# Attention scores with keys on partitions, and two heads side by side on 64 rows of TensorE

## The chip, the cores and the metric

The kernel runs on one core of one Trainium2 chip. The metric is the device time of one execution in microseconds (us), and a lower number is better. One profiled execution, taken by the hardware profiler, gives the trace from which all rows below come.

## The reference

One layer of a hybrid encoder is computed for one sequence of 1024 tokens with 1024 features, in float32. A gated linear recurrence (branch A) and an attention (branch B) are projected from the same normed input, each is gated and projected, their sum goes through an output projection, and a convolutional feed-forward block follows. The change touches the attention alone, which has 8 query heads of 64 features, 2 key/value heads, and no mask:

```python
def gqa_bidirectional(aq, ak, av, q_norm_g, k_norm_g):
    ...
    q = apply_axial_rope(q, tabs) * (AT_HD ** -0.5)
    k = apply_axial_rope(k, tabs)
    ...
    def block(qblk):
        s = jnp.einsum('bqkgd,bskd->bkgqs', qblk, k)
        p = jax.nn.softmax(s, axis=-1)
        return jnp.einsum('bkgqs,bskd->bqkgd', p, v)
```

So every query's scores against all 1024 keys are computed, their maximum is taken off, the exponential is taken, divided by its sum, and multiplied with the values.

## The kernel before

Precision: the TensorE products run on the type `float32r`, which drops low bits of a float32. So each float32 operand is kept as two such halves, a high one (h) and a low one (l), and a product is summed from several partial products. `split` (L76) makes the halves: ScalarE copies the source to h (L77), VectorE subtracts h from the source to get l (L78). `mm3` (L91) issues the products hh, hl and lh.

Order of the stages: projections and the recurrence; the query, key and value projections with their normalisation and rotation (`rope_unit`, L455), from which `finish_q` (L505) and `finish_k` (L496) make transposed halves; the attention; the gated projections of the two branches (L639 on); the output projection; the feed-forward block.

Before the change, `qT[h]` (L427) holds one head: 64 rows of high halves above 64 rows of low halves. `kT[g][0]` holds a key head's high halves twice, one copy below the other, `kT[g][1]` the low halves twice. So one matmul over 128 rows sums two partial products at once.

The attention goes over 32 units (L589 to L603). A unit is a pair of heads (four pairs) and a block of 128 queries (eight blocks). `scores(u, j)` (L540) computes, for one head j of the pair, the scores of 128 queries (on the partitions) against 1024 keys (along a row): four matmuls of 512 columns (L547, L548). VectorE takes each row's maximum (L550), ScalarE the exponential with the maximum as bias and the row sum as a by-product (L553), VectorE the reciprocal (L554), and VectorE scales the row (L555). `turn(u, j)` (L558) then transposes the probabilities on TensorE, eight blocks of 128x128 (L567), because the product with the values needs the keys on partitions, and splits the transposed blocks into halves. `values(u)` (L570) multiplies them with `vv`, which holds for each key block the high and the low half of the values side by side: 16 matmuls of 256 columns (L578). The two halves' results are added (L582 to L586).

TensorE's order is pinned by hand (`pin`, L532). Between these steps `fill(n)` (L535) issues the next n matmuls of ten branch-gate projections (`gate_steps`, L249; 48 matmuls of 512 columns each), which depend on nothing in the attention. The other engines' order is set by the scheduler of the framework, and the DMAs are issued from one queue (SP). PSUM has 8 banks; pool `gps` holds three of them for projections.

## Time and profile before

| what | us |
|---|---|
| median of 3 runs (1615.79 to 1616.55) | 1616.35 |
| the profiled execution | 1616.18 |
| its span, first to last instruction | 1614.3 |
| attention, from the first score matmul (469.5) to the first gated projection (764.5) | 295.0 |

A row of the timeline or of a group names the engine (PE is TensorE's matmuls, PEld its weight loads, DVE is VectorE, ACT is ScalarE, SP issues DMAs), the line of the kernel, the operation, the tiles as out<-in, and the shapes. A matmul's "128\*128 128x512" is the weights' rows and columns and then the output's partitions and columns; the time given for a matmul is a modelled latency, and since matmuls are pipelined, what one costs in a stream is the distance from its start to the next one's.

### The profile page before, as it was taken

How to read it: one execution, taken by the hardware profiler on the slowest of the kernel's cores; microseconds unless marked ns; L12 is line 12 of the kernel's file. 1: busy time of each engine (PE TensorE's matmuls, PEld its weight loads, DVE VectorE, ACT ScalarE, POOL GpSimd, SP SyncE). 2: the span in 40 equal slices, each digit the busy share in tenths (PEclk: the TensorE clock that was granted, in tenths of full speed). 3: DMA queues.
4: the chain of work that ended last, by engine and by line, in shares of the span. 5: the costliest groups of instructions: out<-in, count | busy, mean ns of one | idle time of the engine just before them, and what ended most of it. 6: DMA issues, size and time to landing. Idle time of an engine off the chain costs nothing.

```text
span 1614.3 us, 21171 instructions
## 1 busy us (share of the span) xinstructions
PE 1579.3 (98%) x8376; PEld 1334.1 (83%) x8376; DVE 1112.5 (69%) x1632; ACT 768.0 (48%) x1204; POOL 35.3 (2%) x33
## 2 busy tenths in 40 slices
PE   8999999999999999999999989999999999999998
PEld 7988998888988888888788877788788888787887
DVE  5366465534758888888654288887888777967576
ACT  5375454513555666656432344544544444444432
POOL 0000000000000000000000052000000000000000
PEclk9999999999999999999999999999999999999999
DMA  5011111121110101102445111322222224685343
GB/s 204 27 41 38 53 40 49 64 78 54 46 60 27 46 33 40 47 26 99 167 140 195 53 59 66 104 98 98 98 98 98 103 106 147 212 296 186 100 122 104
DMA packets 59764, 150.34 MB, mean 93 GB/s; under 512 B 6161, under 2 KB 6417, under 8 KB 59666
## 3 DMA queue, kind: packets, MB, share of 16 engines
q1 hardware_dynamic: 59666, 148.99, 26.9%
q8 instruction: 66, 1.08, 0.3%
q14 instruction: 32, 0.26, 0.1%
HBM read 109.91 MB, written 39.06 MB: 92 GB/s over the span
## 4 chain that ended last, share of the span: by engine, by line
PE 85%; DVE 6%; DMA 5%; ACT 3%; issue 1%; SPq 0%; DVEq 0%; ACTq 0%
PE pa L741 13%; PE gp L257 10%; PE pc L741 6%; PE pv L578 4%; PE pb L741 3%; PE pt L567 3%; PE s L547 2%; PE hp L93 2%; PE s L548 2%; PE hp L94 2%; PE hp L92 2%; PE y L93 2%; PE y L94 2%; PE y L92 2%; PE wo L94 2%; PE wo L93 2%
## 5 line engine op out<-in xcount | busy, mean ns | idle before, releaser
L77 ACT CAST pth<-pt 128x512 fp32r<-128x512 f32 x128 | 71.1, 589 | 77.8 <-PE pt L567 77.5
L77 ACT CAST dz<-dr 128x512 fp32r<-128x512 f32 (+1 forms) x66 | 50.6, 767 | 102.1 <-PE da L94 35.8
L78 DVE TENSOR_TENSOR dz<-dr,dz 128x512 fp32r<-128x512 f32 (+1 forms) x66 | 56.9, 867 | 50.8 <-ACT dz L77 50.6
L78 DVE TENSOR_TENSOR ptl<-pt,pth 128x512 fp32r<-128x512 f32 x128 | 84.0, 683 | 10.3 <-ACT pth L77 9.9
L257 PE MATMUL gp<-uT1h,w_g 128*128 128x512 f32 x256 | 86.9, 398 | 0.0
L257 PE MATMUL gp<-uT0h,w_g 128*128 128x512 f32 x256 | 86.4, 400 | 0.0
L550 DVE TENSOR_REDUCE m<-s 128x1 f32<-128x1024 f32 x64 | 78.3, 1224 | 7.3 <-PE s L548 6.3
L553 ACT ACTIVATE p<-s,m 128x1024 f32<-128x1024 f32 x64 | 72.1, 1127 | 19.7 <-DVE m L550 19.7
L741 PE MATMUL pc<-c1t,wb 128*128 128x512 f32 x264 | 69.5, 398 | 5.5 <-ACT c1t L77 5.0
L741 PE MATMUL pa<-c0b,wa 128*128 128x512 f32 x264 | 68.9, 394 | 2.8 <-ACT wa L77 1.7
L741 PE MATMUL pb<-c0b,wa 128*128 128x512 f32 x264 | 68.7, 390 | 0.5 <-DVE ta L714 0.5
L567 PEld LDWEIGHTS pt<-cs,p 128*128 128x128 f32 x512 | 58.7, 140 | 12.0 <-issue 4.8
L741 PE MATMUL pa<-c1t,wb 128*128 128x512 f32 x264 | 67.9, 395 | 0.0
L567 PE MATMUL pt<-cs,p 128*128 128x128 f32 x512 | 66.9, 273 | 0.5 <-DVE p L555 0.5
L578 PE MATMUL pv<-pth,vv 128*128 128x256 f32 x256 | 65.1, 292 | 0.0
L741 PEld LDWEIGHTS pc<-c1t,wb 128*128 128x128 f32 x264 | 50.5, 192 | 17.0 <-ACT c1t L77 5.2
L77 ACT CAST wc<-r 128x1024 fp32r<-128x1024 f32 x22 | 23.1, 1052 | 86.1 <-PE pc L741 76.4
L578 PE MATMUL pv<-ptl,vv 128*128 128x256 f32 x256 | 62.5, 282 | 0.0
L741 PEld LDWEIGHTS pa<-c0b,wa 128*128 128x128 f32 x264 | 49.0, 188 | 15.4 <-ACT wa L77 3.2
L741 PEld LDWEIGHTS pa<-c1t,wb 128*128 128x128 f32 x264 | 50.1, 190 | 12.0 <-DVE c1t L78 0.4
L741 PEld LDWEIGHTS pb<-c0b,wa 128*128 128x128 f32 x264 | 49.5, 188 | 11.4 <-DVE ta L714 0.9
L868 DVE SCALAR_TENSOR_TENSOR cv<-c,vc,cv 128x1023 f32<-128x1023 f32 x44 | 56.3, 1279 | 2.6 <-ACT cv L867 2.6
(461 smaller groups left out, 4578.1 us busy)
## 6 DMA issues: line engine op xcount, KB each, us to landing
r<-in_wup_dram SPq DMA_DIRECT2D x44, 512.0 KB, 3.3
left_d<-cv SPq DMA_DIRECT2D x33, 512.0 KB, 3.2
dr<-left_d SPq DMA_DIRECT2D x66, 256.0 KB, 2.7
raw_g<-in_win_f_dram SPq DMA_DIRECT2D x16, 512.0 KB, 3.2
gate_d<-gt SPq DMA_DIRECT2D x32, 256.0 KB, 2.0
gl<-gate_d SPq DMA_DIRECT2D x16, 512.0 KB, 4.0
raw_h<-in_win_f_dram SPq DMA_DIRECT2D x12, 512.0 KB, 3.3
w<-in_wdown_dram SPq DMA_DIRECT2D x20, 256.0 KB, 5.4
```

The costliest lines, as they stand in the source:

```text
L77: S.copy(h, src)
L78: V.tensor_tensor(out=l, in0=src, in1=h.bitcast(F32), op=ALU.subtract)
L92: T.matmul(ps, ah, bh, start=first, stop=False, skip_group_check=more)
L93: T.matmul(ps, ah, bl, start=False, stop=False, skip_group_check=more)
L94: return T.matmul(ps, al, bh, start=False, stop=last, skip_group_check=more)
L257: yield T.matmul(ps, a[:, w], b[:, k, :], start=k == 0 and n == 0, stop=k == KT - 1 and n == 2)
L550: V.tensor_reduce(out=m, in_=s, axis=AX.X, op=ALU.max, negate=True)
L553: S.activation(pb, s, AF.Exp, bias=m, accum_out=z)
L567: pin(T.transpose(pt[:, i, :], pb[:, k * P:(k + 1) * P], ident))
L578: pin(T.matmul(pv, vv[pair // 2][:, k, :], pts[u][k // 4][n][:, k % 4, :, :], start=k == 0 and n == 0, stop=k == KT - 1 and n == 1))
L741: T.matmul(ps, a[:, k * P:(k + 1) * P], x[:, k, :], start=first and n == 0, stop=n == len(seq) - 1, skip_group_check=not first)
L868: V.scalar_tensor_tensor(out=cv[:, 1:], in0=src[:, :-1], scalar=w0, in1=cv[:, 1:], op0=ALU.mult, op1=ALU.add)
```

## The change

The scores are computed the other way round, with 128 keys on the partitions and 512 queries along a row, so that no probabilities need transposing. `qT[pair]` now is a high tile and a low tile, each with the pair's first head on rows 0 to 63 and its second head on rows 64 to 127; `finish_q` splits per pair. The attention is 8 units u (a pair and a half of the queries) of 8 steps n (a block of 128 keys):

- `maxima(n)` is a first pass with queries on partitions, on the high halves alone: two matmuls of 64 rows, one per head, and a VectorE maximum over 2x512. After eight of these, `max_row(u)` transposes the maxima into one row per head (partitions 0 and 64). The first pass runs 12 steps ahead (`LEAD`).
- `scores(n)` issues three partial products (hh, lh, hl) for each of the two heads, on 64 rows each, and then for each head a matmul of one row of ones with the row of negated maxima, which subtracts the maximum. ScalarE takes the exponential of both heads, and `split` makes the halves.
- `values(n)` multiplies with the values, four matmuls of 512 columns over all 128 rows, and VectorE adds the step's probabilities to a running sum.
- `norm(u)`, ten steps later, sums that over the partitions with four matmuls against ones; the sums go through DRAM (`z_d`), are inverted, come back spread over partitions, and scale the output of a pair. It is run for every unit; the trip to DRAM and back is made once per pair.
- `fill` is called with 6 after each of the first 12 maxima, 10 before the loop, 3 and 2 in each step, 24 after it, and the rest behind the last `norm`.
- The PSUM pool `gps` is closed ahead of the attention and its work there goes through two banks of `mps`; the pool `mp` of the stage behind is opened only when the attention's own pool is closed.

The functions `scores`, `turn` and `values` of before and their loop are removed; three places where a `gps.tile` call is written as `psg` are left out below.

```diff
@@ -57,9 +57,11 @@
     dram = ctx.enter_context(tc.tile_pool(name="dram", bufs=1, space=bass.MemoryType.DRAM))
     gstack = ExitStack()
     gps = pool("gps", 3, gstack, space=PSUM)
+    psg = lambda name: gps.tile([P, 512], F32, tag="g", name=name)
     oa_d = dram.tile([HG_HEADS, P, L], F32, name="oa_d")
     gate_d = dram.tile([2 * KT, P, L], F32, name="gate_d")
+    z_d = dram.tile([4, 2, 2, L], F32, name="z_d")
     h_d = dram.tile([8, P, D], F32, name="h_d")
     left_d = [dram.tile([7, P, NH], F32, name=f"left_d{k}") for k in range(NFF // 2)]
@@ -424,7 +426,7 @@
     slot_q = lambda name, dt=F32R: slot(apq, "q", 8, name, dt)
     slot_k = lambda name, dt=F32R: halves(apk.tile([P, 2, L], dt, tag="k", name=name, bufs=2))
     slot_v = lambda name, dt=F32R: halves(apk.tile([P, 2, L], dt, tag="v", name=name))
-    qT = [slot_q(f"qT{h}") for h in range(AT_HEADS)]
+    qT = [[slot_q(f"q{n}{r}") for n in "hl"] for r in range(AT_HEADS // 2)]
     kT = [slot_k(f"kT{g}") for g in range(2)]
     vv = [v.rearrange("p (a b) -> p a b", b=P) for v in slot_v("vv")]
@@ -504,30 +506,39 @@
     def finish_q(base):
         def f(a, t0, n, name):
-            st = rp.tile([P, 4, n, 2, HD], F32R, tag="st", name=f"st{name}{t0}", bufs=2)
-            split(st[:, :, :, 0, :], st[:, :, :, 1, :], a)
-            for h in range(4):
-                transposed(st[:, h].rearrange("p n a e -> p n (a e)"), qT[base + h], t0, n, f"{name}{h}{t0}")
+            st = rp.tile([P, 2, 2, n, 2, HD], F32R, tag="st", name=f"st{name}{t0}", bufs=2)
+            for r in range(2):
+                both = lambda z: z.rearrange("p n a e -> p a n e")
+                split(both(st[:, 0, r]), both(st[:, 1, r]), a[:, 2 * r:2 * r + 2])
+                for z in range(2):
+                    transposed(st[:, z, r].rearrange("p n a e -> p n (a e)"), qT[base + r][z], t0, n, f"{name}{z}{r}{t0}")
         return f
     rope_unit(unit_t(4, "kv"), 2, tabs[1], finish_k, "k", vsplit=True)
     rope_unit(unit_t(5, "q0"), 4, tabs[0], finish_q(0), "q0")
-    end = rope_unit(unit_t(6, "q1"), 4, tabs[0], finish_q(4), "q1")
+    end = rope_unit(unit_t(6, "q1"), 4, tabs[0], finish_q(2), "q1")
     with tc.issue_after(end.ins):
         for c in range(NG0, NG0 + NG1):
             gate_proj(c)
     pr.close()
-    mn = ExitStack()
-    mp = pool("mp", 1, mn, side="right")
+    gstack.close()
+    mn, ob0 = ExitStack(), ExitStack()
+    mo = pool("mo", 1, ob0, side="right")
+    slot_o = lambda name, dt=F32R: slot(mo, "ob", 1, name, dt)
+    ast = ExitStack()
+    mp = pool("mpa", 1, ast, side="right")
     mps = pool("mps", 1, at, space=PSUM)
-    slot_t = lambda name, dt=F32R: slot(mp, "pt", 8, name, dt)
-    slot_p = lambda name, dt=F32R: slot(mp, "p", 2, name, dt)
-    slot_o = lambda name, dt=F32R: slot(mp, "ob", 1, name, dt)
+    psg = lambda name: mps.tile([P, 512], F32, tag="g", name=name, bufs=2)
+    ps2 = lambda name: mps.tile([P, 2, 512], F32, tag="s", name=name, bufs=2)
     obT = []
-    probs, pts = {}, {}
     fills = (m for c in range(NG0 + NG1, 2 * KT) for m in gate_steps(c))
+    NU = 8
+    heads = (slice(0, HD), slice(HD, P))
     def pin(ins):
         tc.keep_in_program_order(ins)
@@ -536,75 +547,139 @@
         for m in itertools.islice(fills, n):
             pin(m)
...
+    mneg, mrow = {}, {}
+    def maxima(n):
+        u, qt, hf = n // 8, n % 8 // 2, n % 2
+        pair, c = u // 2, u % 2
+        if n % 8 == 0:
+            mneg[u] = mp.tile([P, 4, 2, 2], F32, tag="mneg", name=f"mneg{u}", bufs=2)
+        o = c * 512 + qt * P
+        ps = ps2(f"x{n}")
+        for i, r in enumerate(heads):
+            pin(T.matmul(ps[:, i, :], qT[pair][0][r, o:o + P], kT[pair // 2][0][r, hf * 512:(hf + 1) * 512],
+                         start=True, stop=True))
+        V.tensor_reduce(out=mneg[u][:, qt, hf, :], in_=ps, axis=AX.X, op=ALU.max, negate=True)
+        if n % 8 == 7:
+            V.tensor_tensor(out=mcol[:, :, 0:HD + 1:HD], in0=mneg[u][:, :, 0, :], in1=mneg[u][:, :, 1, :], op=ALU.min)
+    def max_row(u):
+        pt = psg(f"mt{u}")
+        for t in range(4):
+            pin(T.transpose(pt[0:HD + 1, t * P:(t + 1) * P], mcol[:, t, :], ident))
+        mrow[u] = mp.tile([P, 512], F32R, tag="mrow", name=f"mrow{u}", bufs=2)
+        S.copy(mrow[u][0:HD + 1, :], pt[0:HD + 1, :])
+    probs, accs = {}, {}
+    def scores(n):
+        u, kt = n // 8, n % 8
+        pair, c = u // 2, slice(u % 2 * 512, u % 2 * 512 + 512)
+        kh, kl = (z[:, kt * P:(kt + 1) * P] for z in kT[pair // 2])
+        qh, ql = qT[pair]
+        ps = ps2(f"s{n}")
+        for j, (a, b) in enumerate(((kh, qh[:, c]), (kh, ql[:, c]), (kl, qh[:, c]), (ones, mrow[u]))):
+            for i, r in enumerate(heads):
+                w = slice(r.start, r.start + 1) if j == 3 else r
+                pin(T.matmul(ps[:, i, :], a[w, :], b[w, :], start=j == 0, stop=j == 3))
+        p = mp.tile([P, 2, 512], F32, tag="p", name=f"p{n}", bufs=5)
+        S.activation(p, ps, AF.Exp)
+        ph, pl = (mp.tile([P, 2, 512], F32R, tag=f"p{z}", name=f"p{z}{n}", bufs=2) for z in "hl")
+        split(ph, pl, p)
+        probs[n] = ph, pl, p
+    def add_to(acc, p):
+        V.tensor_tensor(out=acc, in0=acc, in1=p, op=ALU.add)
+    pvs = {}
+    def values(n):
+        u, kt = n // 8, n % 8
+        pair = u // 2
+        if kt == 0:
+            pvs[u] = [mps.tile([P, 512], F32, tag="v", name=f"pv{u}{i}", bufs=2) for i in range(2)]
+            if u % 2 == 0:
+                obT.append((slot_o if pair == 0 else slot_q)(f"obT{pair}", F32))
+        for i in range(2):
+            for z, p in enumerate(probs[n][:2]):
+                pin(T.matmul(pvs[u][i], vv[pair // 2][:, kt, :], p[:, i, :], start=kt == 0 and z == 0, stop=kt == 7 and z == 1))
+        p = probs.pop(n)[2]
+        if kt == 0:
+            accs[u] = p
         else:
-            fill(8)
+            add_to(accs[u], p)
+        if kt < 7:
+            return
+        c = slice(u % 2 * 512, u % 2 * 512 + 512)
+        f = mp.tile([P, 512], F32, tag="f", name=f"f{u}")
+        for i, r in enumerate(heads):
+            S.copy(f[r, :], pvs[u][i][heads[1 - i], :])
+        for i, r in enumerate(heads):
+            V.tensor_tensor(out=obT[pair][r, c], in0=pvs[u][i][r, :], in1=f[r, :], op=ALU.add)
+    def norm(u):
+        pair, c = u // 2, slice(u % 2 * 512, u % 2 * 512 + 512)
+        ah, al = (mp.tile([P, 2, 512], F32R, tag=f"p{z}", name=f"a{z}{u}", bufs=2) for z in "hl")
+        split(ah, al, accs.pop(u))
+        z = psg(f"z{u}")
+        for i in range(2):
+            for j, a in enumerate((ah, al)):
+                pin(T.matmul(z, side[:, (1 - i) * P:(2 - i) * P], a[:, i, :], start=i + j == 0, stop=i + j == 2))
+        zs = mp.tile([P, 512], F32, tag="f", name=f"zs{u}")
+        S.copy(zs, z)
+        for i in range(2):
+            nc.sync.dma_start(z_d[pair, 0, i:i + 1, c], zs[i * HD:i * HD + 1, :])
+        if u % 2 == 0:
+            return
+        rz = mp.tile([P, 16], F32, tag="rz", name=f"rz{u}")
+        flat = lambda a: a.rearrange("i (p w) -> (i p) w", w=16)
+        nc.sync.dma_start(rz, flat(z_d[pair, 0]))
+        V.reciprocal(rz, rz)
+        nc.sync.dma_start(flat(z_d[pair, 1]), rz)
+        rb = mp.tile([P, L], F32, tag="p", name=f"rb{u}", bufs=5)
+        for i, r in enumerate(heads):
+            nc.sync.dma_start(rb[r, :], z_d[pair, 1, i:i + 1, :].to_broadcast([HD, L]))
+        V.tensor_tensor(out=obT[pair], in0=obT[pair], in1=rb, op=ALU.mult)
+    one_f = mp.tile([P, 512], F32, tag="f", name="one_f")
+    nc.gpsimd.memset(one_f[:, 0:4 * HD], 0.0)
+    nc.gpsimd.memset(one_f[:, HD:3 * HD], 1.0)
+    side = mp.tile([P, 4 * HD], F32R, name="side")
+    S.copy(side, one_f[:, 0:4 * HD])
+    ones = side[:, HD:3 * HD]
+    mcol = mp.tile([P, 4, HD + 1], F32, name="mcol")
+    nc.gpsimd.memset(mcol, 0.0)
+    LEAD = 12
+    for n in range(LEAD):
+        maxima(n)
+        fill(6)
+        if n == 8:
+            max_row(0)
+    scores(0)
+    fill(10)
+    for n in range(8 * NU):
+        if n + 1 < 8 * NU:
+            scores(n + 1)
+        fill(3)
+        if n + LEAD < 8 * NU:
+            maxima(n + LEAD)
+        values(n)
+        if n % 8 == 2 and n > 8:
+            norm(n // 8 - 1)
+        if (n + LEAD) % 8 == 0 and n + LEAD < 8 * NU + 8:
+            max_row((n + LEAD) // 8 - 1)
         fill(2)
-        if u + 1 < NU:
-            scores(u + 1, 0)
-        fill(4)
-        turn(u, 1)
-        fill(PER - 6)
+    fill(24)
+    norm(NU - 1)
     fill(10000)
-    values(NU - 1)
+    ast.close()
     at.close()
     mid.close()
+    mp = pool("mp", 1, mn, side="right")
+    slot_t = lambda name, dt=F32R: slot(mp, "pt", 8, name, dt)
+    slot_p = lambda name, dt=F32R: slot(mp, "p", 2, name, dt)
     cst_ = ExitStack()
@@ -612,7 +687,7 @@
     xs2 = lambda t: cp.tile([P, D], F32, tag="xs", name=f"xs2{t}", bufs=1)
     cols = lambda tag, name: tuple(cp.tile([P, KT, 512], F32R, tag=tag, name=f"{name}{n}") for n in "hl")
     yst = ExitStack()
-    yps = pool("yps", 5, yst, space=PSUM)
+    yps = pool("yps", 6, yst, space=PSUM)
     oab = []
     for h in range(HG_HEADS):
         t = slot_p(f"oal{h}", F32)
@@ -660,7 +735,6 @@
     yst.close()
-    gstack.close()
     ust, fst = ExitStack(), ExitStack()
     fps = pool("fps", 1, fst, space=PSUM)
     bank = lambda tag, n, name: fps.tile([P, 512], F32, tag=tag, name=name, bufs=n)
@@ -818,6 +892,7 @@
         m1(j)
         m2(j)
     mn.close()
+    ob0.close()
     kst.close()
```

## Rows read from the trace of the kernel before

**Rows 1.** The page's busy time per engine, and granted TensorE clock in 40 slices.

```profile
PE 1579.3 (98%) x8376; PEld 1334.1 (83%) x8376; DVE 1112.5 (69%) x1632; ACT 768.0 (48%) x1204; POOL 35.3 (2%) x33
PEclk9999999999999999999999999999999999999999
```

**Rows 2.** Windows: stretch, its length, each engine's busy time and instructions, clock, DMA share, GB/s.

```profile
core 0: us, PE busy (x) PEld busy (x) DVE busy (x) ACT busy (x) POOL busy (x), PEclk, DMA share, GB/s
469.50:764.50 295.00, 292.98 (x1760) 251.49 (x1761) 243.16 (x395) 180.31 (x352) 0.00 (x0) 0.99 0.13 44
```

**Rows 3.** Groups by line, 469.5 to 764.5: count | busy us, mean ns | idle before.

```profile
L78 DVE TENSOR_TENSOR ptl<-pt,pth 128x512 fp32r<-128x512 f32 x128 | 84.0, 683 | 10.3 <-ACT pth L77 9.9
L550 DVE TENSOR_REDUCE m<-s 128x1 f32<-128x1024 f32 x64 | 78.3, 1224 | 7.3 <-PE s L548 6.3
L553 ACT ACTIVATE p<-s,m 128x1024 f32<-128x1024 f32 x64 | 72.1, 1127 | 19.7 <-DVE m L550 19.7
...
L567 PE MATMUL pt<-cs,p 128*128 128x128 f32 x512 | 66.9, 273 | 0.5 <-DVE p L555 0.5
L578 PE MATMUL pv<-pth,vv 128*128 128x256 f32 x256 | 65.1, 292 | 0.0
...
L78 DVE TENSOR_TENSOR w_g<-raw_g,w_g 128x1024 fp32r<-128x1024 f32 x7 | 8.5, 1221 | 1.1 <-ACT w_g L77 1.1
...
L77 ACT CAST w_g<-raw_g 128x1024 fp32r<-128x1024 f32 x7 | 7.4, 1056 | 3.3 <-PE gp L257 3.1
```

**Rows 4.** Timeline of PE over one unit: start, us, what; [idle before].

```profile
627.82 1.04 PE L567 MATMUL pt<-cs,p 128*128 128x128 f32 x8
628.61 0.36 PE L578 MATMUL pv<-pth,vv 128*128 128x256 f32 x1
...
630.61 0.62 PE L257 MATMUL gp<-uT0h,w_g 128*128 128x512 f32 x2
631.07 0.39 PE L547 MATMUL s<-kT,qT 128*128 128x512 f32 x1
631.30 0.39 PE L548 MATMUL s<-kT,qT 128*128 128x512 f32 x1
...
637.37 0.36 PE L578 MATMUL pv<-pth,vv 128*128 128x256 f32 x1
```

**Rows 5.** Timeline of PE in the recurrence, where 64-column weight tiles alternate with full ones.

```profile
128.79 0.43 PE L359 MATMUL a<-qd,k 128*128 128x64 f32 x2
129.06 0.39 PE L360 MATMUL a<-qd,k 128*128 128x64 f32 x2
129.38 0.27 PE L361 MATMUL a<-qd,k 128*64 128x64 f32 x1
129.39 0.27 PE L362 MATMUL a<-qd,k 128*64 128x64 f32 x1
129.49 0.22 PE L361 MATMUL a<-qd,k 128*64 128x64 f32 x1
129.49 0.22 PE L362 MATMUL a<-qd,k 128*64 128x64 f32 x1
129.64 0.43 PE L359 MATMUL a<-qd,k 128*128 128x64 f32 x2
...
130.35 0.22 PE L362 MATMUL a<-qd,k 128*64 128x64 f32 x1
130.50 0.50 PE L93 MATMUL hp<-uT1l,w_h 128*128 128x512 f32 x1
130.83 0.39 PE L94 MATMUL hp<-uT1h,w_h 128*128 128x512 f32 x1
```

**Rows 6.** Timeline of PE, six matmuls of 128 columns with their weight loads.

```profile
126.00 0.83 PE L338 MATMUL u<-vt,kT 128*128 128x128 f32 x6
```

**Rows 7.** Timeline of DVE, two instructions of 1024 columns back to back.

```profile
753.02 1.22 DVE L550 TENSOR_REDUCE m<-s 128x1 f32<-128x1024 f32 x1
754.16 1.22 DVE L78 TENSOR_TENSOR ob<-obT,ob 128x1024 fp32r<-128x1024 f32 x1
```

**Rows 8.** DMA issues, 469.5 to 780: count, KB each, us to landing.

```profile
gate_d<-gt SPq DMA_DIRECT2D x20, 256.0 KB, 2.0
...
oal<-oa_d SPq DMA_DIRECT2D x4, 512.0 KB, 4.0
```

**Rows 9.** Timeline behind the attention, weight loads and matmuls: two idle times of TensorE.

```profile
766.26 0.19 PEld L92 LDWEIGHTS y<-oah,w_ab 128*128 128x128 f32 x1 [0.53 <-ACT oah L77]
...
767.52 0.50 PE L93 MATMUL y<-oal,w_ab 128*128 128x512 f32 x1 [0.77 <-DVE oal L78]
```

More of the change, by code (lines that the diff above doesn't have):

```diff
@@ L251, in gate_steps @@
         for half in range(2):
-            ps = gps.tile([P, 512], F32, tag="g", name=f"gp{c}{half}")
+            ps = psg(f"gp{c}{half}")
             h, l = uT[half]
@@ L537, in fill @@
             pin(m)
-    def scores(u, j):
-        pair, qt = u // 8, u % 8
-        g, h = pair // 2, 2 * pair + j
-        qs = slice(qt * P, (qt + 1) * P)
-        s = mps.tile([P, L], F32, tag="s", name=f"s{u}_{j}")
-        for hf in range(2):
-            w = slice(hf * 512, (hf + 1) * 512)
-            pin(T.matmul(s[:, w], qT[h][:, qs], kT[g][0][:, w], start=True, stop=False))
-            pin(T.matmul(s[:, w], qT[h][:, qs], kT[g][1][:, w], start=False, stop=True))
-        m = mp.tile([P, 1], F32, tag="m", name=f"m{u}_{j}", bufs=3)
-        V.tensor_reduce(out=m, in_=s, axis=AX.X, op=ALU.max, negate=True)
-        pb = slot_p(f"p{u}_{j}", F32)
-        z = mp.tile([P, 1], F32, tag="z", name=f"z{u}_{j}", bufs=3)
-        S.activation(pb, s, AF.Exp, bias=m, accum_out=z)
-        V.reciprocal(z, z)
-        V.tensor_scalar_mul(pb, pb, z)
-        probs[u, j] = pb
@@ L570, in values @@
-    def values(u):
-        pair, qt = u // 8, u % 8
-        if qt == 0:
-            obT.append((slot_o if pair == 0 else slot_q)(f"obT{pair}", F32))
-        qs = slice(qt * P, (qt + 1) * P)
-        pv = mps.tile([P, 256], F32, tag="v", name=f"pv{u}")
-        for k in range(KT):
-            for n in range(2):
-                pin(T.matmul(pv, vv[pair // 2][:, k, :], pts[u][k // 4][n][:, k % 4, :, :],
-                             start=k == 0 and n == 0, stop=k == KT - 1 and n == 1))
-        pts.pop(u)
-        f = mp.tile([P, P], F32, tag="f", name=f"f{u}", bufs=2)
-        S.copy(f[0:HD, :], pv[HD:P, 0:P])
-        S.copy(f[HD:P, :], pv[0:HD, P:256])
-        for j in range(2):
-            r = slice(j * HD, (j + 1) * HD)
-            V.tensor_tensor(out=obT[pair][r, qs], in0=pv[r, j * P:(j + 1) * P], in1=f[r, :], op=ALU.add)
```

25 lines of the change are left out of this document (3 added, 22 removed).

## The prediction, made before the changed kernel was run

> **What bounds the kernel now.** I read the page's busy times first: TensorE is busy for 98% of the span at full granted clock (9 in every slice), VectorE for 69%, ScalarE for 48% [rows 1]. An average over stages says little about one stage, so the window of the attention comes next: 295.0 us, of which TensorE is busy 293.0, VectorE 243.2 and ScalarE 180.3 [rows 2]. Busy time of a matmul is a modelled latency, so what it really costs is read from start to start in the timeline of one unit [rows 4]: 16 matmuls of 256 columns take 628.61 to 630.61, 2.00 us; two gate matmuls of 512 columns take 0.46, and a score matmul 0.23; eight transposes take 627.82 to 628.61, 0.79. By these the stage is: 480 fills x 0.23 = 110.4; 256 score matmuls x 0.23 = 58.9; 32 units x 2.00 for the values = 64.0; 64 groups of transposes x 0.79 = 50.6. That is 283.9 of 295.0, and the other 11 are a start at a stall and small waits. So TensorE's own stream sets the time of this stage; VectorE, at 82%, is the next engine.
>
> **The change on TensorE, with nothing lost at its seams.** The transposes go (-50.6). The fills stay (110.4). The values become 64 steps x 4 matmuls x 0.23 = 58.9. The scores become 64 x 8 matmuls, but with only 64 rows (or one) in each, in pairs on different rows of the array. If the two of a pair run side by side, a pair costs one matmul and a little: in the only side-by-side matmuls of this trace, L361 and L362, whose weights take 64 columns each, the second starts 0.01 us behind the first [rows 5]. So I take 0.24 for a pair: 256 x 0.24 = 61.4. The first pass is 64 pairs, 15.4. The sums over partitions are 32 matmuls, 7.4, and the transposes of the maxima 32 x 0.11 = 3.5, by six matmuls of 128 columns in 0.83 with 0.28 of that the last one's latency [rows 6]. Sum: 110.4 + 58.9 + 61.4 + 15.4 + 7.4 + 3.5 = 257.0, against 283.9: 27 us less.
>
> **What the seams cost.** The array has to be switched between full tiles and tiles of 64 rows or of one row. No row of this trace shows a 64-row tile; the nearest are the 64-column tiles [rows 5]. A period there, 128.79 to 129.64, is 0.85 us and holds four full-array matmuls, which cost 0.11 each where nothing is switched [rows 6], and two column pairs at 0.10: 0.64. The missing 0.21 is one switch out and one back, so 0.10 for each, with 64 columns streamed. With 512 columns behind it the way back is dearer: from the last tiled matmul (130.35) to the second 512-column one (130.83) is 0.48, where 0.10 + 0.23 = 0.33 would do, so 0.15. On the way out of a 512-column stream I have no row. The 64-column case starts the next shape 0.21 after a matmul of 0.27, most of its latency; a 512-column matmul has a latency of 0.39 and a spacing of 0.23, so up to 0.16. I take 0.14 for each switch, between 0.10 and 0.18 (0.16 and some weight load that no longer hides).
>
> How many: a step goes scores on 64 rows, ones on one row, fill on all, maxima on 64, values on all, which is five switches for the 52 steps that still have a first pass and three for the last 12; the 12 maxima ahead of the loop have two each. 260 + 36 + 24 = 320, and 320 x 0.14 = 44.8 (32 to 58 by the bounds). If the one-row matmuls are no shape of their own it is 256 switches, 35.8.
>
> The Trainium skill speaks against this change here: its page "TensorEngine Tiling (Array Packing)", section "Tiling Modes", says that changing the tiling mode, as opposed to the tile, drains TensorE. The column tiles of rows 5 agree with about 0.10 us; no row shows it for row tiles. By that rule the sum is the forecast; without it, it is rival 1. The same skill's page "TensorE: Matmul & The Clock Gate", Part 3 on packing small matmuls, states that four 32-row matmuls of 512 columns came out 3.07 times faster, not four. By that an estimate of a pair is 1.3 x 0.23 = 0.30, and the forecast would be 320 x 0.06 = 19 us longer.
>
> **VectorE.** A step has a maximum, a subtract and (in seven of eight) an add, all over 1024 columns. Back to back such a pair starts 1.14 us apart, and one lasts 1.22 [rows 7], as the maxima and the gates' subtracts of the whole stage do [rows 3]. So 2.875 x 1.14 = 3.28 for a step. Over eight steps come the split of the sums (1.14), two output adds (0.68 each by the 512-column subtract [rows 3]), half a scaling (0.57) and 0.83 of a gate's split (0.95), which is 0.50 for a step. Total 3.78, or 4.04 if each costs its full 1.22. TensorE's step is 0.96 scores + 1.15 fills + 0.24 maxima + 0.92 values + 0.17 (norm and maxima's row) = 3.44, and 4.14 with five switches. So with switches TensorE still sets the pace, with VectorE at 91%; without them VectorE would. The removed scaling and half-size splits are in this already. ScalarE has an exponential (1.13) and a copy (1.06) per step [rows 3], 53%, and is not near.
>
> **What waits behind what.** `values(n)` waits for VectorE's subtract of step n, and all later matmuls are queued behind it. From the end of `scores(n)` the chain is exponential 1.13, copy 1.06, subtract 1.22, and one foreign VectorE instruction in front, 1.14: 4.5 us. TensorE has between them fills, maxima, values, fills, scores, fills and maxima, 4.2, and eight switches, 1.1: 5.3. It is covered by 0.8; two instructions in front use it up (rival 3). The PSUM slot of the maxima has most of a step for 1.22 us. Of `finish_q`, the second split per call adds a fixed part of some 0.15 on each of ScalarE and VectorE (0.683 at 512 columns against 1.221 at 1024 [rows 3]), eight times, behind projection matmuls: nothing, 0.3 if it delays the first maxima.
>
> **Queues and the end.** `norm` puts on SP, per pair, two stores per unit, a load, a store and two loads, each waiting for the one ahead to land, 2.0 us for the nearest store and 4.0 for the nearest load [rows 8]: 8 to 16 us in which the gate stores and weight loads behind it wait. A gate's weights last 48 fills, some 40 us, so for three pairs that is hidden. For the last pair, copy, four hops, scaling and split are 12 to 20 us; 54 fills (12.4) and the first 21 projection matmuls (4.8) cover 17. Before, two waits for loaded operands, 0.53 and 0.77, stand there already [rows 9]. I add 3 (0 to 12, if the recurrence's loads queue behind the trip).
>
> **The sum.** Made against the profiled execution, 1616.18, which is within 0.2 of the median of the runs, 1616.35; its span is 1614.3, and what lies around it doesn't change. The stage: 257.0 + 44.8 + 9 of the old small losses (the other 2 went with the transposes) + 3 = 313.8, against 295.0: 19 longer, **1635**. With the bounds of the switch, 32 and 58, and 0 to 12 at the end: 1619 to 1657; with 256 switches 1626.
>
> **Rivals.**
> 1. *Row tiles switch almost free.* For it: rows 5 are of column tiles, and with row tiles both shapes write all PSUM partitions. Against: in rows 5 every one of the switches costs the same. Then VectorE is the bound in the loop: 12 x 1.62 + 2.3 + 52 x 3.9 + 12 x 3.20 + 78 fills x 0.23 = 281, and 7 for start and end: 288, **1609** (1603 at 3.78 per step, 1616 at 4.04). This is the faster side: it decides below about 0.08 us per switch.
> 2. *A pair doesn't run side by side.* For it: no row shows 64-row tiles. Against: the 0.01 us of rows 5. Then 320 pairs cost 0.46 instead of 0.24, 70 us: **1705** with the switches, 1660 without them.
> 3. *The chain to `values` is not covered.* VectorE at 91% has two instructions in front, the chain is 5.7 against 5.3, and each of the 52 steps loses 0.4: **1656**. Against: VectorE's order follows readiness, and at 82% of VectorE TensorE lost about 4% [rows 2].
>
> **How the numbers follow.** Forecast with its bounds 45%, rival 1 30%, rival 2 7%, rival 3 8%; in 10% a switch costs 0.08 to 0.10 and all cancels, within 0.2% (3.2 us), which is about what a measurement of this kernel can tell from no change. So faster 0.30, same 0.10, slower 0.60. The forecast's own range is 1619 to 1657. The range of 8 in 10 takes in rival 1 and rival 3 and leaves out rival 2 and the ends: 1603 to 1657.
>
> **What the new profile would show.** Right: pairs of score matmuls 0.01 us apart; a distance of 0.35 to 0.41 instead of 0.23 wherever a matmul of another shape follows; steps of 4.1 to 4.2 us; VectorE with short idle times. Rival 1: 0.23 to 0.28 at the seams, steps of 3.8 to 4.0, TensorE waiting for VectorE's subtract. Rival 2: pairs 0.2 us apart. Rival 3: idle time of TensorE ahead of `values`, released by L78. The forecast is wrong most easily at the switch: each 0.03 us of it is 10 us.

## The result, and the profile after

The changed kernel takes 1698.59 us (median of 3 runs, 1698.33 to 1699.07); the ratio to the kernel before is 1.051, 95% interval 1.0486 to 1.0534. It is slower, as forecast, but by 82 us where 19 were forecast, and above the range.

The profiled execution took 1699.07 us. Its busy times and its granted clock by slices, which answer to [rows 1]:

```profile
PE 1635.7 (96%) x8056; PEld 1287.3 (76%) x8056; DVE 1125.1 (66%) x1480; ACT 771.4 (45%) x1061; POOL 36.1 (2%) x36
...
PEclk9999999999999998998999999999999999999999
```

TensorE's share fell from 98% to 96%, and some slices in the attention show a clock below full speed; before there was none. The windows view of the attention, from its first matmul (469.6) to the first gated projection (847.6), with the columns of [rows 2]:

```profile
469.60:847.60 378.00, 348.79 (x1441) 203.40 (x1440) 255.88 (x237) 183.90 (x205) 0.00 (x0) 0.93 0.12 38
```

378.0 us in place of 295.0: the whole loss is here (1699.1 - 378.0 and 1616.2 - 295.0 are both 1321). TensorE has 29 us without work instead of 2, VectorE falls to 68% and so isn't the bound, and the mean clock is 0.93 instead of 0.99.

**One step.** The timeline of TensorE over one step (start, modelled latency, what; x2 is a pair of matmuls on the two halves of the rows):

```profile
622.01 0.40 PE L259 MATMUL gp<-uT0h,w_g 128*128 128x512 f32 x1
622.34 0.50 PE L584 MATMUL s<-qh,kT 64*128 64x512 f32 x2
622.68 0.39 PE L584 MATMUL s<-ql,kT 64*128 64x512 f32 x2
622.91 0.40 PE L584 MATMUL s<-qh,kT 64*128 64x512 f32 x2
623.24 0.50 PE L584 MATMUL s<-mrow,side 1*128 1x512 f32 x2
623.66 0.50 PE L259 MATMUL gp<-uT0h,w_g 128*128 128x512 f32 x1
624.00 0.39 PE L259 MATMUL gp<-uT0l,w_g 128*128 128x512 f32 x1
624.23 0.40 PE L259 MATMUL gp<-uT0h,w_g 128*128 128x512 f32 x1
624.55 0.50 PE L560 MATMUL x<-kT,qh 64*128 64x512 f32 x2
624.99 0.50 PE L605 MATMUL pv<-ph,vv 128*128 128x512 f32 x1
625.33 0.39 PE L605 MATMUL pv<-pl,vv 128*128 128x512 f32 x1
...
626.58 0.50 PE L584 MATMUL s<-qh,kT 64*128 64x512 f32 x2
```

Read the distances between starts. Two pairs of one shape are 0.23 apart (622.68 to 622.91), as far as two single matmuls (624.00 to 624.23): a pair costs what one matmul costs. At a change of shape the first distance is 0.33 (622.01 to 622.34), and the one behind it as well (0.34, to 622.68). Around a lone pair the two run together: into the ones 0.33, out of them 0.42, and 0.34 behind. A switch lengthens two distances by 0.10 each, some 0.2 in all; five of them make the step 4.24 us (622.34 to 626.58). The median of the first 50 steps is 4.247.

**The sums.** Every unit but the last stops TensorE in the same way. The timeline of all engines at the third unit's `norm`, without weight loads:

```profile
630.03 0.40 PE L605 MATMUL pv<-pl,vv 128*128 128x512 f32 x1
630.23 1.04 ACT L79 CAST ah<-p 128x1024 fp32r<-128x1024 f32 x1
630.48 1.22 DVE L592 TENSOR_TENSOR p<-p,p 128x1024 f32<-128x1024 f32 x1
631.33 0.49 PE L628 MATMUL z<-ah,side 128*128 128x512 f32 x1 [0.90 <-ACT ah L79]
631.61 1.22 DVE L80 TENSOR_TENSOR pl<-p,ph 128x1024 fp32r<-128x1024 f32 x1
632.75 1.22 DVE L80 TENSOR_TENSOR al<-p,ah 128x1024 fp32r<-128x1024 f32 x1
634.02 0.50 PE L628 MATMUL z<-al,side 128*128 128x512 f32 x1 [2.19 <-DVE al L80]
```

The matmuls of the sums (z, L628) are pinned right behind `values(n)`, but their operands come only then: ah and al take the buffers of ph and pl (two of each), which `values(n)` has just read, so ScalarE's copy starts at 630.23 and VectorE's subtract stands behind an add and the step's own subtract. The list of TensorE's waits over the stage:

```profile
PE z L628 <- DVE al L80: 14.1, 7, 2.2
PE z L628 <- ACT ah L79: 6.8, 7, 1.3
PE y L94 <- ACT oah L79: 5.7, 1, 5.7
```

**The clock.** Windows ahead of, at and behind the same place:

```profile
600.00:634.80 34.80, 31.71 (x141) 17.61 (x141) 29.61 (x27) 18.77 (x20) 0.00 (x0) 0.99 0.11 32
634.80:645.00 10.20, 9.95 (x28) 5.17 (x26) 3.66 (x4) 3.14 (x4) 0.00 (x0) 0.50 0.07 27
645.00:679.20 34.20, 31.10 (x139) 17.23 (x135) 28.09 (x25) 19.75 (x22) 0.00 (x0) 1.00 0.12 39
```

For 10.2 us behind the wait the granted clock is 0.50 (1.2 GHz), and TensorE starts 28 matmuls in them, where 34.8 us at the full level hold 141. There are eight such stretches, 3.4 to 10.2 us long, 61.2 us together, each at the end of a stop of TensorE or right behind it: seven at the sums, 54.4 us, and one at the end, 6.8, which lies mostly behind the stage.

**The end.** The timeline there:

```profile
841.53 0.39 PE L259 MATMUL gp<-uT1h,w_g 128*128 128x512 f32 x1
841.70 1.23 DVE L643 TENSOR_TENSOR obT<-obT,rb 128x1024 f32<-128x1024 f32 x1 [7.67 <-DMA rb<-z_d]
...
842.99 0.80 SPq L694 DMA_DIRECT2D oal<-oa_d  x2
...
847.60 0.80 PE L94 MATMUL y<-oah,w_ab 128*128 128x512 f32 x1 [5.69 <-ACT oah L79]
848.19 0.63 PE L94 MATMUL y<-ob,w_ab 128*128 128x512 f32 x1
848.62 0.63 PE L95 MATMUL y<-ob,w_ab 128*128 128x512 f32 x1
```

The load of branch A's heads (oal) is issued only when the last pair has been scaled, since its tiles lie in the memory of the attention's pool; TensorE has no fills left, waits 5.69, and then its matmuls are 0.43 apart instead of 0.23. So of each microsecond at half level (0.43 - 0.23)/0.43, some 0.46 by the unrounded starts, is lost; 0.45 is taken below.

**The account of the stage.** A wait is counted from start to start, less the 0.23 of a matmul: 630.03 to 631.33 and to 634.02 is 3.52 for a unit (2.8 for the seventh), 23.9 for the seven; 5.8 at the end; 2.4 for the others of the list. With 257.0 of work as in the forecast, 320 switches x 0.195 = 62.4, and 54.4 x 0.45 = 24.5 for the clock that is 376.0, against 378.0. The 2 us that are left were not traced to a place.

### The profile page after: what moved, and what is told of

It is laid out like the page before. It is cut to its first block, busy times and chain, and to the rows that moved or that the text cites. A ratio compares the mean times of both kernels' runs of the same rounds, so it can differ in the third digit from the quotient of the medians.

```text
span 1696.9 us, 20241 instructions
## 1 busy us (share of the span) xinstructions
PE 1635.7 (96%) x8056; PEld 1287.3 (76%) x8056; DVE 1125.1 (66%) x1480; ACT 771.4 (45%) x1061; POOL 36.1 (2%) x36
## 4 chain that ended last, share of the span: by engine, by line
PE 84%; DVE 7%; DMA 4%; ACT 2%; issue 2%; SPq 0%; DVEq 0%; ACTq 0%
PE pa L815 13%; PE gp L259 10%; PE pc L815 6%; PE s L584 5%; PE pv L605 4%; PE pb L815 3%; PE y L94 2%; PE y L96 2%; PE y L95 2%; PE hp L95 2%; PE hp L96 2%; PE hp L94 2%; PE x L560 2%; PE wo L94 2%; PE wo L96 2%; PE wo L95 2%
## 5 line engine op out<-in xcount | busy, mean ns | idle before, releaser
L586 ACT ACTIVATE p<-s 128x1024 f32<-128x1024 f32 x64 | 65.7, 1027 | 113.4 <-PE s L584 113.3
L562 DVE TENSOR_REDUCE mneg<-x 128x2 f32<-128x1024 f32 x64 | 78.3, 1224 | 43.2 <-PE x L560 43.0
L259 PE MATMUL gp<-uT1h,w_g 128*128 128x512 f32 x256 | 94.0, 422 | 0.2 <-ACT zs L630 0.2
L592 DVE TENSOR_TENSOR p<-p,p 128x1024 f32<-128x1024 f32 x56 | 68.2, 1218 | 30.1 <-ACT p L586 29.8
L80 DVE TENSOR_TENSOR pl<-p,ph 128x1024 fp32r<-128x1024 f32 x64 | 78.0, 1219 | 7.1 <-ACT ph L79 7.1
L79 ACT CAST ph<-p 128x1024 fp32r<-128x1024 f32 x64 | 67.3, 1051 | 1.8
L259 PEld LDWEIGHTS gp<-uT1h,w_g 128*128 128x128 f32 x256 | 49.0, 195 | 16.6 <-issue 7.0
L584 PE MATMUL s<-qh,kT 64*128 64x512 f32 x256 | 61.6, 477 | 0.0
L259 PEld LDWEIGHTS gp<-uT0h,w_g 128*128 128x128 f32 x256 | 48.2, 192 | 16.8 <-issue 7.1
L605 PE MATMUL pv<-ph,vv 128*128 128x512 f32 x128 | 59.3, 464 | 0.0
```

The source lines that it names most:

```text
L79: S.copy(h, src)
L80: V.tensor_tensor(out=l, in0=src, in1=h.bitcast(F32), op=ALU.subtract)
L259: yield T.matmul(ps, a[:, w], b[:, k, :], start=k == 0 and n == 0, stop=k == KT - 1 and n == 2)
L562: V.tensor_reduce(out=mneg[u][:, qt, hf, :], in_=ps, axis=AX.X, op=ALU.max, negate=True)
L584: pin(T.matmul(ps[:, i, :], a[w, :], b[w, :], start=j == 0, stop=j == 3))
L586: S.activation(p, ps, AF.Exp)
```

## The experiments

The theory tested: the stage is slow by switches of 0.195 us, by the sums' stop, by the half clock behind it, and a little by the end. The rivals: the pairs don't really share the array (the result lies near that rival's 1705), or the step is set by VectorE or by the chain to `values`. "Step" below is the median distance, over the first 50 steps, from one step's first `values` matmul to the next one's; the half clock is summed over the stage and its end. The kernel before, against which each ratio goes, took 1613.7 to 1616.5 in the median beside the different groups of runs, so 2 or 3 us between two kernels of the table say little; the columns behind the ratio come from one traced execution each, which can lie 4 us off the median.

| kernel | us | ratio to before, 95% | stage us | half clock us | switches in a step | step us |
|---|---|---|---|---|---|---|
| changed kernel | 1698.6 | 1.0486 to 1.0534 | 378.0 | 61.2 | 5 | 4.247 |
| e1 sums' own buffers | 1675.0 | 1.0349 to 1.0384 | 356.5 | 34.0 | 5 | 4.247 |
| e2 ones on 64 rows | 1682.9 | 1.0405 to 1.0436 | 366.8 | 54.4 | 4 | 4.061 |
| e3 maxima behind scores | 1692.2 | 1.0457 to 1.0505 | 374.2 | 54.4 | 4 | 4.053 |
| e4 all three | 1641.2 | 1.0140 to 1.0174 | 320.4 | 23.8 | 2 | 3.662 |
| e5 full rows | 1703.3 | 1.0524 to 1.0559 | 385.1 | 44.2 | 0 | 4.407 |
| e6 more switches | 1765.0 | 1.0912 to 1.0945 | 444.5 | 102.5 | 9 | 5.040 |
| e7 halves of reciprocals | 1629.3 | 1.0065 to 1.0100 | 312.0 | 13.6 | 2 | 3.941 |
| e8 busy in the wait | 1704.8 | 1.0533 to 1.0570 | 385.7 | 44.4 | 5 | 4.247 |
| e9 early loads | 1623.9 | 1.0038 to 1.0072 | 305.1 | 3.4 | 2 | 3.948 |
| e10 half the adds on GpSimd | 1634.2 | 1.0093 to 1.0130 | 314.1 | 13.6 | 2 | 3.959 |
| e11 without the adds | 1627.5 | 1.0060 to 1.0093 | 306.7 | 13.6 | 2 | 3.662 |
| e12 fills spread anew | 1623.6 | 1.0049 to 1.0077 | 304.7 | 3.4 | 2 | 4.045 |

### e1: the sums' split in buffers of its own, and earlier

```diff
+    def norm_split(u, i):
+        halved[u] = [mp.tile([P, 512], F32R, tag=f"a{z}", name=f"a{z}{u}{i}", bufs=1) for z in "hl"]
+        split(*halved[u], accs[u][:, i, :])
...
-        ah, al = (mp.tile([P, 2, 512], F32R, tag=f"p{z}", name=f"a{z}{u}", bufs=2) for z in "hl")
-        split(ah, al, accs.pop(u))
...
+        if n % 8 == 7:
+            norm_split(n // 8, 0)
+        if n % 8 == 1 and n > 8:
+            norm_sum(n // 8 - 1, 0)
+            norm_split(n // 8 - 1, 1)
...
```

> The edit: the sums' halves get buffers of their own (one head at a time, 512 columns each; the pool of p goes from 5 to 4 buffers to make room) and are split one to two steps ahead of the matmuls that read them, instead of taking the buffers of ph and pl that the step just behind frees. Theory A (the changed kernel's 82 us are: TensorE waiting some 24 us for the split inside norm, some 25 us lost to the half clock that follows each of these waits, 18 us more at the switches than forecast, 6 to 9 at the end): both the waits ahead of z and the half-clock stretches between 545 and 810 go, 1698.6 - 49 = 1650 (1643 to 1660). Theory B (row-tile pairs don't run side by side, 70 us): only the 24 us of waits go, 1675, and half-clock stretches stay. Theory C (VectorE is the bound of the loop): the split costs VectorE the same wherever it stands, so under 10 us are gained.

1675.0, 23.6 us gained: the number that theory B gave, but not by its way. The waits ahead of z are gone, and the step is unchanged. But more than half of them came back in another place, 14.4 us ahead of `values` (the buffers of p are four here, not five, to make room). Rows of the timeline at the first of these places:

```profile
590.00 0.58 ACT L571 CAST mrow<-mt 65x512 fp32r<-65x512 f32 x1 [4.10 <-PE mt L569]
...
594.26 1.21 DVE L592 TENSOR_TENSOR p<-p,p 128x1024 f32<-128x1024 f32 x1
596.33 1.22 DVE L650 TENSOR_TENSOR obT<-obT,rb 128x1024 f32<-128x1024 f32 x1 [0.85 <-DMA rb<-z_d]
597.47 2.35 DVE L80 TENSOR_TENSOR pl<-p,ph 128x1024 fp32r<-128x1024 f32 x2
598.74 0.80 PE L605 MATMUL pv<-pl,vv 128*128 128x512 f32 x1 [4.43 <-DVE pl L80]
```

ScalarE waited 4.10 for the row of maxima with the next exponential behind it, and on VectorE the scaling of a finished pair, which waits for its DMA, stands ahead of the step's subtract. TensorE waits 4.43 ahead of `values`. At three such places 27.2 us at half clock remain of 54.4 (34.0 with the end). So the sums' stop was real, and the step that the forecast feared in rival 3 is next in line.

### e2 and e3: one switch fewer in a step

```diff
 # e2
...
-                w = slice(r.start, r.start + 1) if j == 3 else r
-                pin(T.matmul(ps[:, i, :], a[w, :], b[w, :], start=j == 0, stop=j == 3))
+                pin(T.matmul(ps[:, i, :], a[r, :], b[r, :], start=j == 0, stop=j == 3))
...
 # e3
             scores(n + 1)
-        fill(3)
         if n + LEAD < 8 * NU:
             maxima(n + LEAD)
+        fill(3)
```

> The edit: the matmuls that subtract the maxima read 64 rows (63 of them zero) instead of one, so they have the same shape as the scores ahead of them; 320 switches of shape become 256. Theory A: the 0.09 us from a 64-row matmul to a one-row one goes 64 times, and if leaving a one-row shape costs more than leaving 64 rows, a little more: 1686 to 1693. Theory B (pairs not side by side, switches cheap): no change, 1697 to 1700.

> The edit: in a step the maxima stand right behind the scores and the three fills behind them, so one trip out of the full shape is saved (the one-row matmuls still stand between: four switches for five). Theory A: 52 x 0.2 = 10 us less, 1688 (1684 to 1694). Theory B: no change. Theory C: the maxima come earlier in the step but VectorE's work is the same, no change.

In e2 the row of negated maxima lies in 64 rows with zeros below it. The matmuls stay, but a one-row matmul is no longer a shape of its own: the step falls by 0.186, the time by 15.7, which is more than the 6 to 13 expected (in the traced execution the stage is 11.2 shorter). In e3 the step falls by 0.194 as well, but the time only by 6.4: the profile shows 9.1 us of waits of `values` for VectorE's pl, where the changed kernel has 1.0.

### e4: the three together

> The three edits together: two switches per step instead of five (152 in all instead of 320), and no wait for the split in norm. Theory A: 1698.6 - 49 - 168 x 0.2 = 1616 (1606 to 1630), level with the kernel before, with steps of about 3.9 to 4.0 us, where VectorE's 3.8 to 4.0 begins to show. Theory B: 1675 or more. Theory C: no better than the first of these.

1641.2, 57.4 us gained, more than the three gains one by one (45.7); the step is 3.662. It is above the expectation: 9.6 us of waits for pl, up to 4.6 each, and the 5.9 of the end remain.

### e5 and e6: no row tiles, and more switches

```diff
 # e5, on e2's form
...
-                pin(T.matmul(ps[:, i, :], a[r, :], b[r, :], start=j == 0, stop=j == 3))
+                pin(T.matmul(ps[:, i, :], a, b, start=j == 0, stop=j == 3))
 # e6
                 pin(T.matmul(ps[:, i, :], a[w, :], b[w, :], start=j == 0, stop=j == 3))
+            if n and j < 3:
+                fill(1)
...
-        fill(3)
+        else:
+            fill(3)
```

> The form with 64 ones per head, but the matmuls of the maxima and of the three score products read all 128 rows instead of 64, so no matmul of the attention is a row tile and no pair shares the array; the two heads' scores come out summed, so the separation of the two heads is left out. Against that form (1682.9): theory A (a pair runs side by side for 0.235 us, and each of 256 switches costs 0.195): 256 switches go, -50; 320 pairs become two matmuls of 0.23 one after the other, +72; 1700 to 1710. Theory B (pairs did not really run side by side, the stage is slow for that): nothing is lost, the switches alone go, about 1633 or less. Theory C (a switch costs nothing, the excess is all waits): +72, 1755.

> The changed kernel with the same matmuls in another order: the three fills that stand in a step behind the ones go one each behind the first three pairs of scores, so a step has nine switches between shapes instead of five (four more in 63 steps). Theory A (0.195 us per switch): 252 x 0.195 = +49, 1748 (if 0.14 as forecast: +35, 1734). Theory B (switches are cheap; the excess is waits and half clock): under +8, 1699 to 1707.

e5 comes out at 1703.3, within 2 us of the sum by the theory; 64 steps that are 0.346 longer than e2's give 22 us, and the time grew by 20. No switch is left and yet the step is longer, 4.407, which is 19 matmuls at 0.232: ten one after the other instead of five pairs, and the nine others. That settles rival 2: were the pairs not side by side, taking the switches away would have gained 50 us. e6 has the changed kernel's matmuls in another order:

```profile
644.57 0.50 PE L584 MATMUL s<-qh,kT 64*128 64x512 f32 x2
645.00 0.50 PE L259 MATMUL gp<-uT0h,w_g 128*128 128x512 f32 x1
645.43 0.50 PE L584 MATMUL s<-ql,kT 64*128 64x512 f32 x2
645.87 0.50 PE L259 MATMUL gp<-uT0l,w_g 128*128 128x512 f32 x1
646.29 0.50 PE L584 MATMUL s<-qh,kT 64*128 64x512 f32 x2
```

Every distance is 0.43 where it would be 0.23, at full clock. The steps of the table lie on a line: 3.662 with two switches, 4.06 with four, 4.247 with five, 5.040 with nine; from two to nine that is 1.378/7 = 0.197 for each. It leads back to 3.27 without any, which is the forecast's 3.44 less the 0.17 of `norm` and maxima's row. e6 is 17 us above its expectation, and 41 us more at half clock (x 0.45 = 18.5) account for that: the stops are as long as before, but the low level lasts up to 20.5 us behind them.

### e8: TensorE busy while it waits

```diff
         z = psg(f"z{u}")
+        for i in range(14 if u < NU - 1 else 0):
+            pin(T.matmul(z, side[:, 0:P], uT[0][0][:, i % KT, :], start=True, stop=True))
```

> The changed kernel with 14 useless full-array matmuls of 512 columns (3.2 us) ahead of the sums' matmuls of the first seven units, in the place where TensorE waits for the split of the sums, so that it is busy there instead of idle; nothing is left out. The wait itself stays as long. Theory A (the idle waits are what the half granted clock follows, and it costs 0.46 us for each us at it): 51 of the 61 us at half clock go, -23; 1673 to 1680. Theory B (the half clock has another cause, or costs nothing because TensorE waits anyway): 1695 to 1705 with the half clock as before.

1704.8: no gain, the number of theory B. The trace says otherwise of the clock, though. TensorE at the sums, the window behind them, and VectorE at another place:

```profile
633.03 3.43 PE L627 MATMUL z<-uT0h,side 128*128 128x512 f32 x14
636.29 0.39 PE L630 MATMUL z<-ah,side 128*128 128x512 f32 x1
```

```profile
633.00:650.00 17.00, 16.45 (x76) 9.85 (x74) 10.79 (x11) 7.67 (x9) 0.00 (x0) 1.00 0.04 16
```

```profile
599.94 1.23 DVE L645 TENSOR_TENSOR obT<-obT,rb 128x1024 f32<-128x1024 f32 x1 [1.01 <-DMA rb<-z_d]
601.08 1.22 DVE L80 TENSOR_TENSOR pl<-p,ph 128x1024 fp32r<-128x1024 f32 x1
```

With TensorE busy the clock stays at 1.00 behind the sums, at all four units whose sums don't end a pair. At the three that do, the scaling that waits for its DMA now stands ahead of pl, the next matmul of `values` starts 4.5 to 5.3 us behind the one ahead of it, and 10.2 to 13.7 us at half clock come with that stop. The run shows where the low level comes from and where it doesn't; that removing it alone saves time it doesn't show, since new stops of 17.5 us took back what it gave.

### e7 and e9: the buffer of the reciprocals, and the loads at the end

```diff
 # e7, on e4
-        rb = mp.tile([P, L], F32, tag="p", name=f"rb{u}", bufs=4)
...
+        for k, t in enumerate("hl"):
+            rb = mp.tile([P, 512], F32, tag=f"a{t}", name=f"rb{t}{u}", bufs=1)
...
 # e9, on e7
+        if h < 2:
+            t = slot_q(f"oal{h}")
+            nc.sync.dma_start(t.bitcast(F32), oa_d[h])
...
```

> The version with all three edits, and the spread reciprocals in two tiles of 512 columns that take the buffers of the sums' split, so that none of the four buffers of the probabilities is held while the sums go to DRAM and back. Theory A (that holding causes the 13.5 us in which TensorE waits ahead of the values and most of the 23.8 us at half clock there): 1641.2 - 13.5 - 0.46 x 17 = about 1620 (1614 to 1626); with the wait at the end gone too, 1612. Theory B (the waits come from the chain scores, exponential, copy, subtract itself): no change, 1638 to 1644.

> The version with the reciprocals in halves (1629.3), and the first two heads of branch A loaded behind the attention into tiles of the queries' pool, which come free with the last scores, instead of the memory of the attention's own pool. Theory A (the 6.3 us in which TensorE waits ahead of the first gated projection come from these loads, issued at 772.59 behind the reciprocals' way back): the wait goes, and the 6.8 us at half clock behind it with their 3 us; 1618 to 1623. Theory B (what is late next is as late: the other two heads and the last scaled pair need the same memory or the same way back, and stand a few matmuls later): 1626 to 1631.

e7: 1629.3, 12 us gained of the 21 expected. The longest wait ahead of `values` falls from 4.6 to 1.1. Its median step of 3.94 is not a slower step. Of the first 50, 24 are at 3.66 (26 in e4, whose median is therefore 3.66); 13 are at about 4.1, and those hold two matmuls of the sums or the transposes of the maxima; 11 are longer than 4.2. The median falls into the gap between these groups, as it does in e9 and e10. The expectations of e10, e11 and e12 take it for the length of a step.

e9: 1623.9, a little outside its range. The wait at the end is gone and with it the half clock there, so the loads were its cause. No form was faster than this one by more than the scatter, and it is still 0.4 to 0.7% slower than the kernel before.

### e10, e11 and e12: is VectorE the bound now?

```diff
 # e10, on e7
-        V.tensor_tensor(out=acc, in0=acc, in1=p, op=ALU.add)
+        V.tensor_tensor(out=acc[:, 0, :], in0=acc[:, 0, :], in1=p[:, 0, :], op=ALU.add)
+        nc.gpsimd.tensor_tensor(out=acc[:, 1, :], in0=acc[:, 1, :], in1=p[:, 1, :], op=ALU.add)
 # e11, on e7
-            add_to(accs[u], p)
+            add_to(accs[u], p) if kt == 1 else None
 # e12, on e9
...
-        fill(2)
+        fill(2 + (n % 2 and n + LEAD < 8 * NU))
```

> The version with the reciprocals in halves (1629.3), and of each running sum of probabilities the second head's 512 columns added by GpSimd, the first head's by VectorE. Theory A (in that version VectorE sets the step: 58.4 of the 60 us from 500 to 560 busy, steps of 3.94 against TensorE's 3.66): VectorE's step falls by some 0.5, TensorE sets the pace at 3.66; 0.28 x 40 steps = 11 us gained, 1616 to 1622. Theory B (VectorE doesn't set the step): no change, 1627 to 1631. Theory C (the two engines slow each other, or GpSimd, which took 2.0 us for such an instruction in the feed-forward block, holds the buffers too long): slower, 1632 to 1650.

> The version with the reciprocals in halves (1629.3), with the running sums of probabilities left out behind the second of a unit's eight key blocks (48 of 56 VectorE adds; the softmax is then divided by a partial sum). It measures by itself what VectorE's adds cost there. Theory A (VectorE sets the step there): steps of 3.66, 10 to 14 us gained, with the remaining waits ahead of the values up to 18; 1611 to 1620. Theory B (TensorE sets the step): no change, 1627 to 1631.

> The version with the early loads (1623.9), with its fills spread anew: ahead of the loop the first pass goes in pairs of maxima with ten fills behind each pair (six fewer pairs of switches there), and the 12 fills saved there and 14 from behind the last step go one each into every second step that has a first pass. Theory A (switches cost 0.195 each wherever they stand, and in the steps of 3.95 VectorE sets the pace, so that more fills there cost nothing): 12 x 0.195 = 2.3 and up to 26 x 0.23 = 6 gained; 1616 to 1620, level with the kernel before. Theory B (TensorE sets the pace in those steps): the fills only change places; 1621 to 1624.

The windows from 500 to 560 us of e7 and of e11:

```profile
500.00:560.00 60.00, 59.53 (x314) 40.42 (x314) 58.38 (x56) 41.64 (x47) 0.00 (x0) 1.00 0.09 31
```

```profile
500.00:560.00 60.00, 59.53 (x314) 40.36 (x312) 46.68 (x44) 41.25 (x48) 0.00 (x0) 1.00 0.09 31
```

In this stretch the two engines are both full in e7 (TensorE 59.53, VectorE 58.38), and with the adds gone TensorE issues the same 314 matmuls: here VectorE's load costs nothing. In some steps behind a finished unit it does: of the first 50 steps 7 are longer than 4.2 in e11 where 11 were, 28 are at 3.66 where 24 were, and the stage of the traced execution is 5.3 us shorter. The time fell by only 2 us, within what the runs scatter, which is the number of theory B: TensorE sets the pace in most steps, VectorE in a few, and what that costs is 5 us at most. e12, which puts more fills into the steps, gains nothing (1623.6): its first passes go in pairs with fewer switches, but a step that gets a fill is longer by it (12 of the first 50 are at 3.89), and the wait for PSUM banks of the fills grows from 2.3 to 3.9 us. Theory B was right there too.

e10 took 5 us more than e7, which is theory C's range, though the intervals of the two ratios still touch. Its groups of the adds, and one step of them:

```profile
L592 POOL TENSOR_TENSOR p<-p,p 128x512 f32<-128x512 f32 x56 | 78.9, 1409 | 294.1 <-ACT p L585 282.2 <-DVE obT L618 11.9
...
L591 DVE TENSOR_TENSOR p<-p,p 128x512 f32<-128x512 f32 x56 | 71.3, 1274 | 4.6 <-ACT p L585 4.4
```

```profile
641.86 1.30 POOL L592 TENSOR_TENSOR p<-p,p 128x512 f32<-128x512 f32 x1 [2.34 <-ACT p L585]
642.26 1.45 DVE L591 TENSOR_TENSOR p<-p,p 128x512 f32<-128x512 f32 x1
```

VectorE's add of 512 columns takes 1.27 us on average, as long as the whole 1024 did alone (1.22). In the same trace the 6 of the 56 adds during which GpSimd added nothing took 0.68 in the mean, and the 44 that overlapped GpSimd's for more than half their time took 1.42. The half that was handed over cost VectorE what it saved.

## Why the prediction was wrong

**The steps that failed.** Three terms make up the miss. The price of a switch was too small, by 17.6 us in all, and two terms were put at nothing: the wait of the sums' matmuls for their operands (23.9) and the half clock behind a stop (24.5). With the switch at its measured price and all else as forecast the time would be 1635 + 17.6 = 1653, still inside the range; the two terms put at nothing carried it out.

**What held.** The direction; the work without seams, 257 us, which the line through the steps bears out; the pair at the price of one matmul; the count of 320 switches with a one-row matmul as a shape of its own (e2 removes one per step); the exclusion of VectorE and of the chain as bounds in the changed kernel (VectorE 68% busy, 1.0 us of waits ahead of `values`). VectorE's step was forecast at 3.78 to 4.04 and is somewhat shorter: in the window of e7 VectorE is busy for 97% of the time, the first 16 steps are 3.81 in the mean, and by these it needs some 3.7.

**The price of a switch was mis-sized:** 0.195 us where 0.14 was taken, with 0.18 as the upper end: 17.6 us. What failed is the reading of [rows 5] on the way out of a 512-column stream, which no row showed: the forecast looked for one lengthened distance and bounded it by a latency. With 512 columns there are two lengthened distances, each by 0.10. The second stood in the rows (130.50 to 130.83 is 0.33 for a 0.23 matmul) and was counted for the way back alone. The Trainium skill, "TensorEngine Tiling (Array Packing)", section "Tiling Modes", says that changing the mode drains TensorE; the lines of e6 agree, with 0.20 for each. The Trainium skill's packing figure on "TensorE: Matmul & The Clock Gate", Part 3, four 32-row matmuls 3.07 times faster, would have made a pair 0.30 by estimate; the 0.23 from pair to pair doesn't bear that out for two tiles of 64 rows.

**What was left out: the stop of the sums.** "What waits behind what" followed the chain to `values`, and "Queues and the end" followed what `norm` puts on SP. `norm`'s matmuls were counted as work (7.4 us), but not asked when their operands are ready, though the diff shows them pinned behind `values(n)` with a split in the buffers which that step still reads: 23.9 us. e1 took it away by buffers and order together, so which of the two holds the split is not separated; the trace shows both, the copy at the end of the last read and the subtract third in VectorE's queue.

**What was left out: the clock.** It was 9 in every slice before, and the forecast priced a stop of TensorE at its length. A slice is 40 us long, though, and hides a short stretch. The stall at the start of the attention, which the forecast carried over as a small loss, shows one in the trace of before:

```profile
468.35 0.71 PE L493 MATMUL ptq<-cs,stq 128*128 128x128 f32 x4 [1.27 <-ACT qT L494]
...
470.51 0.63 PE L548 MATMUL s<-kT,qT 128*128 128x512 f32 x1
470.94 0.63 PE L257 MATMUL gp<-uT0h,w_g 128*128 128x512 f32 x1
```

From 470.1 to 473.5 the granted clock was at half level there, with matmuls 0.43 apart. In the changed kernel it was so for 3.4 to 10.2 us at each of the seven stops of 2.8 to 3.5 us: 24.5 us, as much as the stops themselves. That the low level comes from the stops, e8 shows; its price is worked out from the distances, and no run removed it alone.

**Smaller terms.** The end cost 5.8 where 3 (0 to 12) was taken, and by another way than those listed: not a late scaled pair, but a load that waits for its memory. The 9 us of old small losses carried over were 2.4. Altogether 313.8 + 17.6 + 23.9 + 24.5 + 2.8 - 6.6 = 376.0.

**The rivals.** The time is near rival 2's 1705 by chance: e5 refutes it. Rival 1's floor, 288 us for the stage, wasn't reached by any form, since two switches per step remain (25 us). Rival 3 costs 1 us here, but its waits ahead of `values` appear in e3 and e4, whose steps are shorter, and in e1, whose step is not. Against it the forecast said that VectorE's order follows readiness; in e1 and e8 a scaling that still waits for its DMA stands ahead of the subtract that TensorE needs.

The best form, e9, has 152 switches: 257.0 + 29.6, which alone is a little longer than the 283.9 of before. There the change exchanges the 27 us of work that it saves for as much and a little more in switches, and loses by that and by what is left of waits. What of those could still go was not found.

## What to carry to other kernels

Count the changes of tile shape on TensorE and give each its price before counting what packed tiles save: here five packed pairs saved 1.14 us in a step (4.407 of e5 less 3.27) and five switches took 0.98. For every matmul that is pinned, ask when its last operand is ready and in whose buffers it lies, not only what it costs. A stop of a few microseconds in a dense matmul stream costs more than its length, because of the clock behind it: about twice in the changed kernel, and nearly three times in e6.
